# Two of four weight sums per seven-product group moved from VectorE into adding DMAs

## The chip, the cores and the metric

The kernel runs on one core of a Trainium2 chip. The time is the device time of one execution in microseconds (us), the median of several runs. Its engines are TensorE (PE, matmuls; PEld its weight loads), VectorE (DVE), ScalarE (ACT), GpSimd (POOL) and SyncE (SP, which here only issues DMAs); 16 DMA engines move data between HBM and the on-chip memory SBUF. Each engine takes its instructions in a fixed order, written when the kernel is built, and waits on semaphores for the others.

## The reference

One layer of an encoder, on 512 tokens of width 2048, in float32:

```python
h = layer_norm(x, ln_in_g, ln_in_b)
z = h @ w_in                       # then latent attention and a gated recurrence: y_attn, y_lru
y = concat([y_attn, y_lru]) @ w_out
h = layer_norm(ALPHA * h + y, ln1_g, ln1_b)
f = square(relu(h @ w_up)) @ w_down        # w_up 2048 x 8192, w_down 8192 x 2048
h = layer_norm(ALPHA * h + f, ln2_g, ln2_b)
```

The change concerns the last product pair, `w_up` and `w_down`.

## The kernel before

**Arithmetic.** TensorE multiplies in a rounded format, so every float32 operand is split into a high part (ScalarE rounds it, L159) and a low part (VectorE subtracts the high part from the operand, L160). One product is then three chains of matmuls: high x high, high x low, low x high. `split` does it for operands, `wsplit` (L839) for weight blocks of 128 x 1024, with the tiles `whi` (3 buffers) and `wlo` (2 and, every third time, 1 more). A `wsplit` is traced at a priority 100 instructions earlier than its place (`PO2`), so that it is put ahead of its product.

**Groups of seven products.** Most of `w_up` and `w_down` goes through a Strassen-Winograd scheme on 2 x 2 blocks: `winograd` (L878) computes a 256 x 512 piece of the result with seven block products in place of eight. The operand sums (tiles B11, B21, B22, T1, T2, T3, X4, each with a high part h and a low part l) are made once per stage and once per chunk; the weight sums are made in every group. A group loads its four weight blocks, slabs 0 to 3, as a11, a21, a22, a12 with plain DMAs on SP (`wload`, L860 to 864, 512 KB each) and forms on VectorE, in place, by `tt` (L876, tile `raw`): a11 - a21 (L891, product T3), a21 + a22 (L894, T1), a22 - (a11 - a21) (L899, T2) and a12 minus that (L903, B22). The products run in the order B11, T3, T1, X4, B21, B22, T2, each 24 matmuls (8 x 3, L866 to 873). Between them ScalarE copies the bank of B11 to s1 (L890) and that of T3 to s7 (L893) before the bank is added to, and `evac` writes the four result blocks.

**Stages.** The up projection has two pieces by the ordinary scheme and 30 groups; `up_out` (L773) then forms differences of the result blocks on VectorE and stores 1 MB to `u_dram`. The down projection has four chunks; in each the first piece is ordinary (`classic`, L760), with 7 groups behind it (6 in the last chunk, whose last piece is written apart). That is 57 groups. At the passage into a chunk `u_load` (L912) reads the operands back from `u_dram` in pieces of 512 KB and splits them, on the same queue and engines as the weights.

**Buffers.** `wraw` (L853) takes a weight block's buffer: of seven blocks in a row three from the pool `wr` (3 buffers, shared with the ordinary pieces) and four from the pool `ws` (4 buffers). The pool `ws` is opened at L835 in the space of R, which is freed at L834 once L827 to 833 have formed the operand sums from it.

**Order.** The framework orders each engine's instructions by priority and by when it expects their inputs, and gives buffers to tiles as they come free; a DMA's issue waits on its queue for its buffer. GpSimd issues no DMA in this kernel.

Of the kernel before, what the change touches and what calls it, by code (L numbers as in the profile page):

```python
# [9 lines left out]
F32 = mybir.dt.float32  # L10
F32R = mybir.dt.float32r
I32 = mybir.dt.int32
AF = mybir.ActivationFunctionType
ALU = mybir.AluOpType
# [4 lines left out]
P = 128  # L19
# [23 lines left out]
PO1, PO2 = 100, 100  # L43
# [5 lines left out]
def body(tc, x, pos, vecs, consts, w_in, w_uq, w_kn, w_v, w_rg, w_out, w_up, w_down, out):  # L49
    nc = tc.nc  # L50
    V, A, T, G = nc.vector, nc.scalar, nc.tensor, nc.gpsimd
# [106 lines left out]
    def split(f, hi, lo):  # L158
        A.activation(hi, f, AF.Copy)  # L159
        V.tensor_tensor(out=lo, in0=f, in1=hi.bitcast(F32), op=ALU.subtract)  # L160
# [363 lines left out]
    for step, what in enumerate(ORDER):  # L524
        c, k = what[0], int(what[1])
# [245 lines left out]
            evac(n, acc)  # L771

    def up_out(ch, o):  # L773
        V.tensor_tensor(out=o[:, 4:7:2, :], in0=o[:, 1:4:2, :], in1=o[:, 0:2, :], op=ALU.subtract)
        V.tensor_tensor(out=o[:, 5, :], in0=o[:, 3, :], in1=o[:, 4, :], op=ALU.subtract)
        V.tensor_tensor(out=o[:, 7, :], in0=o[:, 2, :], in1=o[:, 5, :], op=ALU.subtract)
        nc.sync.dma_start(out=u_dram[ch // 8][:, ch % 8], in_=o)
# [6 lines left out]
    def o_tile():  # L784
        return o_p.tile([P, 8, HS], F32, tag="uo", name="uo", bufs=2)
# [14 lines left out]
    for th in range(2):  # L800
        for k in range(KT):
            b, ws = BLK[k // 8, th], slice((k % 8) * P, (k % 8 + 1) * P)
            for n in range(NG):
                wh, wl = sl[n, k // 8]
                o = acc[n][:, TH[th]]
# [3 lines left out]
    for n in range(NG):  # L809
        up_evac(os_[n // 2], n % 2, acc[n])  # L810
        if n % 2 == 1:
            up_out(n // 2, os_[n // 2])
    for n in range(NG, 2 * NCL):
        if n % 2 == 0 and n > NG:
            os_.append(o_tile())
        acc = ps.tile([P, S], F32, tag="mm", name="mm", bufs=3)
        for hf in range(2):
            wh, wl = slab(w_up[2 * n + hf])
            for j in range(8):
                mm_blocks(acc, wh, wl, hf, j)  # L820
        up_evac(os_[n // 2], n % 2, acc)
        if n % 2 == 1:
            up_out(n // 2, os_[n // 2])
# [3 lines left out]
    for g in range(0, 8, 4):  # L827
        b11, b12 = hv[:, g:g + 4, :HS], hv[:, g:g + 4, HS:]
        b21, b22 = hv[:, 8 + g:12 + g, :HS], hv[:, 8 + g:12 + g, HS:]
        for o, x, y, n in ((b11, b12, b11, "T1"), (b12, b22, b12, "T3"), (b22, b22, b11, "T2"),  # L830
                           (b21, b21, b22, "X4")):
            V.tensor_tensor(out=o, in0=x, in1=y, op=ALU.subtract)
            split(o, oph[n][:, g:g + 4, :], opl[n][:, g:g + 4, :])
    free(r_p)  # L834
    ws_p = pool("ws")  # L835
# [3 lines left out]
    def wsplit(f, n):  # L839
        woff[0] = (32, 0) if n in ("T3", "T1") else FAR  # L840
        with tc.high_priority(offset=PO2):
            w = wsplit_(f)
        woff[0] = FAR
        return w

    def wsplit_(f):
        hi = wtile(wr, "whi", 3)
        lon[0] += 1
        lo = wtile(wr, "wlo", 2) if lon[0] % 3 else wtile(ws_p, "wlo", 1)
        split(f, hi, lo)  # L850
        return hi, lo

    def wraw(k):  # L853
        if k % 7 < 3:
            return wr.tile([P, 1024], F32, tag="raw", name="raw", bufs=3)
        return ws_p.tile([P, 1024], F32, tag="raw", name="raw", bufs=4)

    rawn = [0]

    def wload(src):  # L860
        t = wraw(rawn[0])
        rawn[0] += 1
        nc.sync.dma_start(out=t, in_=src)
        return t

    def product(acc, w, n, first):  # L866
        wh, wl = w
        sk = dict(skip_group_check=not first)
        for j in range(8):
            ws = slice(j * P, (j + 1) * P)  # L870
            T.matmul(acc, wh[:, ws], oph[n][:, j], start=first and j == 0, stop=False, **sk)  # L871
            T.matmul(acc, wh[:, ws], opl[n][:, j], start=False, stop=False, **sk)  # L872
            T.matmul(acc, wl[:, ws], oph[n][:, j], start=False, stop=j == 7, **sk)  # L873

    def tt(o, x, y, op):
        V.tensor_tensor(out=o, in0=x, in1=y, op=op)  # L876

    def winograd(slabs, evac, hook=lambda n: None):  # L878

        a11 = wload(slabs[0])  # L880
        a21 = wload(slabs[2])
        a22 = wload(slabs[3])
        a12 = wload(slabs[1])
        bank = lambda tag, bufs: ps.tile([P, HS], F32, tag=tag, name="st_" + tag, bufs=bufs)
        half = lambda n: ws_p.tile([P, HS], F32, tag=n, name=n, bufs=2)
        a, b, c, d = bank("mm", 3), bank("sc", 2), bank("tr", 3), bank("mm", 3)
        s1, s7 = half("s1"), half("s7")
        product(a, wsplit(a11, "B11"), "B11", True)
        hook("B11")
        A.activation(s1, a, AF.Copy)  # L890
        tt(a11, a11, a21, ALU.subtract)  # L891
        product(b, wsplit(a11, "T3"), "T3", True)
        A.activation(s7, b, AF.Copy)  # L893
        tt(a21, a21, a22, ALU.add)  # L894
        product(c, wsplit(a21, "T1"), "T1", True)
        tt(s7, s7, c, ALU.add)
        product(b, wsplit(a22, "X4"), "X4", False)
        hook("X4")
        tt(a11, a22, a11, ALU.subtract)  # L899
        product(a, wsplit(a12, "B21"), "B21", False)  # L900
        hook("B21")
        evac("c11", a, None)
        tt(a12, a12, a11, ALU.subtract)  # L903
        product(c, wsplit(a12, "B22"), "B22", False)
        hook("B22")
        product(d, wsplit(a11, "T2"), "T2", True)
        tt(s1, s1, d, ALU.add)
        evac("c21", s1, b)
        evac("c12", s1, c)
        evac("c22", s1, s7)  # L910
# [13 lines left out]
    for ch in range(NCL, DFF // 256):  # L924
        o = o_tile()

        def evac(which, x, y):
            t = o[:, 2 * int(which[1]) + int(which[2]) - 3, :]
            if y is not None:
                tt(t, x, y, ALU.add)  # L930
                x = t
            A.activation(t, x, AF.Relu)
            A.activation(t, t, AF.Square)
        winograd([w_up[4 * ch + i] for i in range(4)], evac,
                 *([next_ops(0)] if ch == DFF // 256 - 1 else ()))
        up_out(ch, o)
# [150 lines left out]
```

## Time and profile before

| | |
|---|---|
| median of 3 runs | 1981.27 us (1980.73 to 1982.22) |
| the profiled execution | 1981.16 us |
| its span, first to last instruction | 1979.4 us |
| TensorE, VectorE, ScalarE, GpSimd busy | 1932.1, 1501.8, 1014.6, 18.1 us |
| granted TensorE clock, mean | 0.998 of 2.4 GHz |
| bytes by DMA | 284.19 MB, mean 144 GB/s |

Rows below that name a line, an engine and tiles read `out<-in`; L12 is line 12 of the kernel. A group's `x228 | 278.3, 1221 | 3.6` is the number of instructions, their busy time in us, the mean ns of one, and the engine's idle time ahead of them. A timeline row begins with the start in us from the span's start and the duration; in brackets stands the idle time before it and who ended it. SPq is the queue of SP.

### The profile page before, as it was taken

How to read it: one execution, taken by the hardware profiler on the slowest of the kernel's cores; microseconds unless marked ns; L12 is line 12 of the kernel's file. 1: busy time of each engine (PE TensorE's matmuls, PEld its weight loads, DVE VectorE, ACT ScalarE, POOL GpSimd, SP SyncE). 2: the span in 40 equal slices, each digit the busy share in tenths (PEclk: the TensorE clock that was granted, in tenths of full speed). 3: DMA queues.
4: the chain of work that ended last, by engine and by line, in shares of the span. 5: the costliest groups of instructions: out<-in, count | busy, mean ns of one | idle time of the engine just before them, and what ended most of it. 6: DMA issues, size and time to landing. Idle time of an engine off the chain costs nothing.

```text
span 1979.4 us, 39294 instructions
## 1 busy us (share of the span) xinstructions
PE 1932.1 (98%) x16472; PEld 1899.7 (96%) x16472; DVE 1501.8 (76%) x2151; ACT 1014.6 (51%) x1479; POOL 18.1 (1%) x20
## 2 busy tenths in 40 slices
PE   6999999999999999999999999999999999999997
PEld 6999999888999999999999999999999999999997
DVE  7666655677433598888888888888898888888895
ACT  6565566555222455555555555566464454445453
POOL 1000000000000000000000000000000000000001
PEclk9999999999999999999999999999999999999999
DMA  7222222221333345454444445486364355347332
GB/s 244 96 96 94 91 93 85 65 59 65 107 107 123 115 150 204 156 180 154 179 159 162 176 156 182 153 295 223 118 222 162 107 185 198 109 140 244 100 104 86
DMA packets 113890, 284.19 MB, mean 144 GB/s; under 512 B 10161, under 2 KB 56369, under 8 KB 109617
## 3 DMA queue, kind: packets, MB, share of 16 engines
q1 hardware_dynamic: 113712, 281.68, 41.4%
q8 instruction: 129, 2.11, 0.4%
q14 instruction: 49, 0.39, 0.1%
HBM read 234.19 MB, written 46.14 MB: 142 GB/s over the span
## 4 chain that ended last, share of the span: by engine, by line
PE 88%; DVE 4%; ACT 3%; DMA 2%; issue 2%; POOL 0%; SPq 0%; ACTq 0%; DVEq 0%; POOLq 0%
PE st_mm L871 8%; PE st_mm L872 8%; PE st_mm L873 8%; PE mm L142 7%; PE mm L141 7%; PE mm L140 7%; PE st_tr L873 5%; PE st_sc L873 5%; PE st_sc L871 5%; PE st_tr L872 5%; PE st_tr L871 5%; PE st_sc L872 5%; PE mm L756 1%; PE mm L758 1%; PE mm L757 1%
## 5 line engine op out<-in xcount | busy, mean ns | idle before, releaser
L159 ACT ACTIVATE whi<-raw 128x1024 fp32r<-128x1024 f32 x399 | 423.5, 1063 | 513.5 <-DVE raw L876 251.6
L160 DVE TENSOR_TENSOR wlo<-raw,whi 128x1024 fp32r<-128x1024 f32 x399 | 484.5, 1222 | 129.4 <-ACT whi L159 123.5
L876 DVE TENSOR_TENSOR raw<-raw 128x1024 f32<-128x1024 f32 x228 | 278.3, 1221 | 3.6
L124 DVE TENSOR_TENSOR wlo<-raw,whi 128x1024 fp32r<-128x1024 f32 (+1 forms) x128 | 141.3, 1105 | 160.9 <-PE mm L142 110.3
L121 ACT ACTIVATE whi<-raw 128x1024 fp32r<-128x1024 f32 (+1 forms) x128 | 123.0, 966 | 195.6 <-PE mm L141 160.8
L141 PE MATMUL mm<-hl,whi 128*128 128x256 f32 x704 | 195.3, 277 | 0.0
L142 PE MATMUL mm<-hh,wlo 128*128 128x256 f32 x704 | 195.0, 277 | 0.0
L140 PE MATMUL mm<-hh,whi 128*128 128x256 f32 x704 | 194.7, 277 | 0.1
L140 PEld LDWEIGHTS mm<-hh,whi 128*128 128x128 f32 x704 | 132.2, 188 | 0.3 <-ACT xp L443 0.3
L142 PEld LDWEIGHTS mm<-hh,wlo 128*128 128x128 f32 x704 | 132.2, 188 | 0.1
L141 PEld LDWEIGHTS mm<-hl,whi 128*128 128x128 f32 x704 | 132.2, 188 | 0.0
L871 PE MATMUL st_sc<-X4h,whi 128*128 128x256 f32 x456 | 126.6, 278 | 2.0 <-ACT s L893 2.0
L873 PE MATMUL st_sc<-T3h,wlo 128*128 128x256 f32 x456 | 126.5, 277 | 1.8 <-DVE wlo L160 1.8
L871 PE MATMUL st_tr<-B22h,whi 128*128 128x256 f32 x456 | 126.6, 278 | 1.0 <-ACT whi L159 1.0
L873 PE MATMUL st_tr<-B22h,wlo 128*128 128x256 f32 x456 | 126.2, 277 | 0.7 <-DVE wlo L160 0.7
L871 PE MATMUL st_mm<-B21h,whi 128*128 128x256 f32 x456 | 126.0, 276 | 0.8 <-ACT s L890 0.8
L871 PE MATMUL st_mm<-T2h,whi 128*128 128x256 f32 x456 | 126.0, 276 | 0.4 <-ACT whi L159 0.4
L872 PE MATMUL st_sc<-X4l,whi 128*128 128x256 f32 x456 | 126.3, 277 | 0.0
L873 PE MATMUL st_sc<-X4h,wlo 128*128 128x256 f32 x456 | 126.2, 277 | 0.0
L871 PE MATMUL st_sc<-T3h,whi 128*128 128x256 f32 x456 | 126.1, 277 | 0.0
L872 PE MATMUL st_sc<-T3l,whi 128*128 128x256 f32 x456 | 126.1, 277 | 0.0
L873 PE MATMUL st_mm<-B11h,wlo 128*128 128x256 f32 x456 | 126.0, 276 | 0.0
(443 smaller groups left out, 6462.3 us busy)
## 6 DMA issues: line engine op xcount, KB each, us to landing
raw<-in_w_up SPq DMA_DIRECT2D x128, 512.0 KB, 3.3
raw<-in_w_down SPq DMA_DIRECT2D x128, 512.0 KB, 3.6
u_dram<-uo SPq DMA_DIRECT2D x32, 1024.0 KB, 3.8
raw<-in_w_in SPq DMA_DIRECT2D x50, 512.0 KB, 3.2
raw<-in_w_out SPq DMA_DIRECT2D x32, 512.0 KB, 3.2
X4l<-u_dram SPq DMA_DIRECT2D x18, 512.0 KB, 5.3
x<-in_x SPq DMA_DIRECT2D x8, 512.0 KB, 7.1
h_dram<-hf SPq DMA_DIRECT2D x32, 128.0 KB, 2.1
```

Of the source, the lines that this page charges most:

```text
L121: A.activation(hi[:, :w], raw[:, :w], AF.Copy)
L124: V.tensor_tensor(out=lo[:, :w], in0=raw[:, :w], in1=hi[:, :w].bitcast(F32), op=ALU.subtract)
L140: T.matmul(acc[:, c], wh, xh[:, c], start=first and t == 0, stop=False)
L141: T.matmul(acc[:, c], wh, xl[:, c], start=False, stop=False)
L142: T.matmul(acc[:, c], wl, xh[:, c], start=False, stop=last and t == 1)
L159: A.activation(hi, f, AF.Copy)
L160: V.tensor_tensor(out=lo, in0=f, in1=hi.bitcast(F32), op=ALU.subtract)
L756: T.matmul(o, wh[:, ws], oph[b][:, j], start=first and t == 0, stop=False)
L871: T.matmul(acc, wh[:, ws], oph[n][:, j], start=first and j == 0, stop=False, **sk)
L872: T.matmul(acc, wh[:, ws], opl[n][:, j], start=False, stop=False, **sk)
L873: T.matmul(acc, wl[:, ws], oph[n][:, j], start=False, stop=j == 7, **sk)
L876: V.tensor_tensor(out=o, in0=x, in1=y, op=op)
```

## The change

In each group the sum for T3 is now formed with the other sign, as a21 - a11: ScalarE writes -a11 into a tile of its own, s3n, and a DMA on GpSimd's queue adds slab 2 onto it. The sum for T1 is formed in a tile s1w: a plain DMA on SP loads slab 2, and a DMA on GpSimd's queue adds slab 3. The operand T3 changes its sign to match (B12 - B22), and T2's sum becomes a22 + s3n. Two `tt` of the group go. The raw buffers go from 3 + 4 to 3 + 2, and s3w and s1w have 2 each. `up_out` writes its first pair of differences with two instructions in place of one, for the sign. The descriptor scratch of GpSimd's DMAs is set to 8192 bytes per partition.

```diff
     def up_out(ch, o):
-        V.tensor_tensor(out=o[:, 4:7:2, :], in0=o[:, 1:4:2, :], in1=o[:, 0:2, :], op=ALU.subtract)
+        V.tensor_tensor(out=o[:, 4, :], in0=o[:, 1, :], in1=o[:, 0, :], op=ALU.subtract)
+        V.tensor_tensor(out=o[:, 6, :], in0=o[:, 1, :], in1=o[:, 3, :], op=ALU.subtract)
...
-        for o, x, y, n in ((b11, b12, b11, "T1"), (b12, b22, b12, "T3"), (b22, b22, b11, "T2"),
+        for o, x, y, n in ((b11, b12, b11, "T1"), (b12, b12, b22, "T3"), (b22, b22, b11, "T2"),
...
     def wraw(k):
-        if k % 7 < 3:
+        if k % 5 < 3:
             return wr.tile([P, 1024], F32, tag="raw", name="raw", bufs=3)
-        return ws_p.tile([P, 1024], F32, tag="raw", name="raw", bufs=4)
+        return ws_p.tile([P, 1024], F32, tag="raw", name="raw", bufs=2)
...
         a11 = wload(slabs[0])
-        a21 = wload(slabs[2])
+        s3n = ws_p.tile([P, 1024], F32, tag="s3w", name="s3w", bufs=2)
+        with tc.high_priority(offset=PO2):
+            A.activation(s3n, a11, AF.Copy, scale=-1.0)
+        G.dma_start(out=s3n, in_=slabs[2], accum_op=ALU.add)
+        s1w = ws_p.tile([P, 1024], F32, tag="s1w", name="s1w", bufs=2)
+        nc.sync.dma_start(out=s1w, in_=slabs[2])
+        G.dma_start(out=s1w, in_=slabs[3], accum_op=ALU.add)
         a22 = wload(slabs[3])
         a12 = wload(slabs[1])
...
-        tt(a11, a11, a21, ALU.subtract)
-        product(b, wsplit(a11, "T3"), "T3", True)
+        product(b, wsplit(s3n, "T3"), "T3", True)
         A.activation(s7, b, AF.Copy)
-        tt(a21, a21, a22, ALU.add)
-        product(c, wsplit(a21, "T1"), "T1", True)
+        product(c, wsplit(s1w, "T1"), "T1", True)
...
-        tt(a11, a22, a11, ALU.subtract)
+        tt(a11, a22, s3n, ALU.add)
...
-    nc = _bacc.Bacc("TRN2", target_bir_lowering=False, num_devices=1)
+    nc = _bacc.Bacc("TRN2", target_bir_lowering=False, num_devices=1, dynamic_dma_scratch_size=8192)
```

## Rows read from the trace of the kernel before

**Rows 1.** The page: busy time and share by engine, and the DMA queues.
```profile
PE 1932.1 (98%) x16472; PEld 1899.7 (96%) x16472; DVE 1501.8 (76%) x2151; ACT 1014.6 (51%) x1479; POOL 18.1 (1%) x20
...
q1 hardware_dynamic: 113712, 281.68, 41.4%
```

**Rows 2.** Stretches: busy us (instructions) by engine, granted clock, DMA share, GB/s.
```profile
740.00:1300.00 560.00, 560.00 (x4933) 560.00 (x4932) 470.25 (x557) 304.58 (x494) 0.00 (x0) 1.00 0.48 169
1300.00:1330.00 30.00, 27.80 (x239) 27.19 (x239) 28.00 (x32) 25.92 (x37) 0.00 (x0) 1.00 0.97 344
1460.00:1490.00 30.00, 28.77 (x253) 28.57 (x253) 28.55 (x34) 22.30 (x23) 0.00 (x0) 1.00 0.96 325
1500.00:1600.00 100.00, 100.00 (x883) 100.00 (x882) 85.43 (x105) 42.35 (x49) 0.00 (x0) 1.00 0.34 112
1620.00:1650.00 30.00, 28.80 (x248) 28.21 (x248) 28.72 (x33) 19.98 (x21) 0.00 (x0) 1.00 0.96 332
1770.00:1810.00 40.00, 39.44 (x344) 39.05 (x344) 37.27 (x43) 25.07 (x27) 0.00 (x0) 1.00 0.88 303
```

**Rows 3.** Waits of TensorE in 740 to 1900: us in total, times, longest.
```profile
PE st_sc L871 <- ACT s L893: 2.0, 3, 1.2
PE st_sc L873 <- DVE wlo L160: 1.8, 2, 1.0
PE st_tr L871 <- ACT whi L159: 1.0, 1, 1.0
PE st_mm L871 <- ACT s L890: 0.8, 1, 0.8
PE st_tr L873 <- DVE wlo L160: 0.7, 2, 0.4
PE st_mm L871 <- ACT whi L159: 0.4, 1, 0.4
PE mm L758 <- DVE wlo L124: 0.3, 1, 0.3
```

**Rows 4.** The costliest groups of the page: high parts and weight sums.
```profile
L159 ACT ACTIVATE whi<-raw 128x1024 fp32r<-128x1024 f32 x399 | 423.5, 1063 | 513.5 <-DVE raw L876 251.6
...
L876 DVE TENSOR_TENSOR raw<-raw 128x1024 f32<-128x1024 f32 x228 | 278.3, 1221 | 3.6
```

**Rows 5.** Timeline of TensorE: starts of B11, T3 and the next group's B11.
```profile
1105.02 0.28 PE L871 MATMUL st_mm<-B11h,whi 128*128 128x256 f32 x1
...
1107.75 0.28 PE L871 MATMUL st_sc<-T3h,whi 128*128 128x256 f32 x1
...
1124.10 0.28 PE L871 MATMUL st_mm<-B11h,whi 128*128 128x256 f32 x1
```

**Rows 6.** The same group: ScalarE's high part of T3, and SP's later issues.
```profile
1103.40 1.06 ACT L159 ACTIVATE whi<-raw 128x1024 fp32r<-128x1024 f32 x1 [1.90 <-DVE raw L876]
...
1113.72 0.33 SPq L777 DMA_DIRECT2D u_dram<-uo  x1
1117.23 1.48 SPq L863 DMA_DIRECT2D raw<-in_w_up  x2
```

**Rows 7.** Landing times: all loads of L863, its five of 740.5-746, all of L917.
```profile
DMA to landing us min/median/max: 3.0/3.3/9.1
...
DMA to landing us min/median/max: 3.7/5.3/7.6
...
DMA to landing us min/median/max: 3.4/5.5/8.5
```

**Rows 8.** Start of the stage: SP's wait, the last reader of R, T3's first matmul.
```profile
SPq L863 <- DVE X4l L160: 5.3, 1, 5.3
...
739.33 1.22 DVE L160 TENSOR_TENSOR X4l<-R,X4h 128x1024 fp32r<-128x1024 f32 x1
...
745.23 0.28 PE L871 MATMUL st_sc<-T3h,whi 128*128 128x256 f32 x1
```

**Rows 9.** Timeline of TensorE in the passage at 1300: B21 ahead of X4.
```profile
1301.28 0.28 PE L871 MATMUL st_tr<-T1h,whi 128*128 128x256 f32 x1
...
1304.94 0.39 PE L871 MATMUL st_mm<-B21h,whi 128*128 128x256 f32 x1 [0.77 <-ACT s L890]
...
1305.28 0.33 PE L871 MATMUL st_sc<-X4h,whi 128*128 128x256 f32 x1
```

## The prediction, made before the change was run

> **What bounds the kernel now.** The first view is the page's busy table [rows 1]: TensorE is busy for 98% of the span, VectorE for 76%, ScalarE for 51%, GpSimd for 1%; the DMA engines stand at 41.4% of their time. The change takes work from VectorE and gives some to ScalarE, GpSimd's queue and the DMA engines, so the question is where TensorE waits for VectorE at all. The second view, the table of stretches [rows 2], answers it by stage. The 30 seven-product groups of the up projection fill 740 to 1300 us and a little more; there TensorE is busy for 560.00 of 560.00 us, at a granted clock of 1.00, with VectorE at 84% (470.25 / 560) and the DMA engines at 0.48. The quiet part of the down projection (1500 to 1600) is as full: 100.00 of 100.00. Both stretches hold the same 8.8 matmuls per us, with the DMA share at 0.48 and at 0.34, so the matmul rate does not follow the traffic. Only the four passages into a new 2048-column chunk show idle TensorE: 2.20 us in 1300-1330, 1.23 in 1460-1490, 1.20 in 1620-1650, 0.56 in 1770-1810, with the DMA engines at 0.88 to 0.97 and VectorE at 93 to 96%.
>
> The third view, TensorE's waits in 740-1900 [rows 3], gives the most that can be won: 2.0 + 1.8 + 1.0 + 0.8 + 0.7 + 0.4 + 0.3 = 7.0 us, or 0.35% of the time. Of it 1.8 + 0.7 + 0.3 = 2.8 us wait for VectorE (a low part that is late), 4.2 us for ScalarE (a high part, or the copies of s1 and s7). VectorE's share of the whole kernel is therefore the wrong number to read; these 7.0 us are the right one.
>
> **The change, part by part.** *Removed from VectorE:* two of the four 1024-wide sums in each of 57 groups; 228 of them took 278.3 us, 1221 ns each [rows 4], so 114 x 1.22 = 139 us. They lie beside a TensorE that does not stop, so outside the passages they are worth nothing.
>
> *Added to ScalarE:* one 1024-wide negated copy per group, 57 x 1.06 us (the row of the same shape, 1063 ns [rows 4]) = 61 us. ScalarE is busy for 304.58 of 560 us in the up stage [rows 2], 10.4 of the 19.08 us of a group (1105.02 to 1124.10 [rows 5]); with 11.4 it is still hidden. Without that cover it would cost 61 us.
>
> *Added to DMA:* two adding transfers of 512 KB per group, on GpSimd's queue. The third and fourth plain loads stay (slab 2 now goes to s1w). A plain 512 KB load occupies all 16 engines for 512 KB / (169 GB/s / 0.48) = 1.5 us [rows 2]. No adding transfer is in this trace. Bounds: 1.5 us, as a plain load, and 4.5, if its two reads and its write followed one another; I take 3.0, because its reads are doubled and its writes are not. That is 6 us per group (3 to 9), a share of 0.31: the up stage goes from 0.48 to 0.79 (0.64 to 0.95), the quiet down stage from 0.34 to 0.65. Both stay below 1, so I cost it at nothing there.
>
> *Added wait, steady groups.* ScalarE's negation waits for a11's load, and behind it in ScalarE's queue stand the splits, the evacuations and the copies of s1 and s7; the adding DMA waits for the negation, T3's split for the adding DMA. SP issues a load as soon as a buffer is free [rows 6]: the one at 1117.23 follows the low part that frees a12's buffer, and with five buffers for three loads it is that of a11 two groups on. Its landing at the median of 3.3 us [rows 7] gives 1120.5; negation 1.06, adding transfer 6, so s3n is whole by about 1128. T3's high part is written 4.35 us ahead of its product (1103.40 against 1107.75 [rows 5, 6]); two groups on, that write falls at 1103.40 + 2 x 19.08 = 1141.6. Some 14 us are spare, and s1w, loaded when T1's split frees its buffer, has more. Cost: nothing, covered by that lead. If the lead were gone, each late microsecond would cost 57.
>
> *Start of the stage.* The first group has no lead. Its pool ws reuses the space of R, and SP stood 5.3 us for the last reader of R, the low part of X4 that ends at 740.55 [rows 8]. Before, a11, a21 and a22 of that group lay in the other pool, and T3 began at 745.23 [rows 8]. Now the negation cannot write before 740.6: it ends at 741.7, the adding DMA lands 3.0 to 9.1 us later (the fastest and slowest plain loads of this line [rows 7]), the high part takes 1.06, the low part 1.22, less the 0.23 of two matmuls that need only the high part. I take 6.0 us: the five loads issued at that moment landed in a median of 5.3 [rows 7], and half a load's 1.5 us comes on top for the second read. 741.7 + 6.0 + 1.06 + 0.99 = 749.7, which is 4.5 us late (1.5 to 7.6); T1's sum lands while T3 runs. The Trainium skill (DMA: Bandwidth & Descriptors, Anatomy of one DMA) fits a software-issued DMA with 2.0 us plus bytes / 436 GB/s; with two reads that would be an estimate of 4.4 us, and the start would cost 2.9 and the sum 1.6 less. No row here shows such a DMA; I stay with the rows, since the loads of that moment were slower than a lone one.
>
> *Four passages.* Here the operands of the next chunk are read back, in 512 KB pieces that land after 3.4 to 8.5 us [rows 7], on engines that are already at 0.88 to 0.97. The adding DMAs of the groups behind the passage fall into it and share the same engines: 6 us per group, of which I let half delay the operand loads, 3 us. Against it VectorE has two sums less, 2.4 us, on a path where it is 93 to 96% busy. Net +0.6 each, +2.4 for four (bounds: all 7.0 us of waits gone, or +3 each). The Trainium skill (DMA: Bandwidth & Descriptors, Issuing engines are not separate DMA queues) says the same against this change: transfers from another queue run on the same 16 engines and save only issue time. By it alone, with the whole 6 us counted, the four passages would cost +14.4 and the sum 12 more; the rows of the passages show only 0.6 to 2.2 us of waits at full DMA load, so I keep half.
>
> *Small edits.* The outer sum of the up groups becomes two instructions; some 0.1 us of VectorE, under cover. Buffers: 7 raw become 5 plus 2 + 2; no cost while the lead holds. The smaller scratch moves addresses by a whole 8 KB. The nearest row is the matmul rate, 8.8 per us in two stages that use different tiles [rows 2]: 0, up or down.
>
> **Sum.** Steady groups 0, start +4.5, passages +2.4: +6.9. The profiled execution took 1981.16 us (span 1979.4, 1.8 around it), 0.1 below the median of the three runs, so the forecast is 1981.2 + 6.9 = 1988 us.
>
> **Rivals.** A measurement of this kernel can tell about 0.2%, 4 us, from no change; the bounds are 1977.3 and 1985.2.
>
> *Even.* TensorE fills the start with another product (B21 needs neither sum, 2.7 us), or the adding DMA lands at 3.0; start +1.5, passages 0: 1983. For it: in the passage at 1300 TensorE did begin B21 right after T1, ahead of X4 [rows 9]. Against it: the loads at 740.6 were slow [rows 7]. Chance 0.30.
>
> *Faster.* VectorE's relief clears the passages: its own 2.8 us, and most of the 4.2 behind ScalarE. It decides if the operand loads are not slower than now. 1981.2 + 1.5 - 7.0 = 1976. Against it: ScalarE's waits there are for landings, which get no earlier. Chance 0.14.
>
> *DMA-bound groups.* If an adding transfer holds the engines for 6 us, an up group needs 4 x 1.5 + 2 x 6 + 3 (its 1 MB store) = 21 us against 19.08, and the 30 groups become 30 x 1.9 = 58 us longer: 2040. It decides from (19.08 - 9) / 2 = 5 us per transfer, just above my upper bound of 4.5. The Trainium skill (Collectives: The Full Stack, The bandwidth ceiling) says that an add in the DMA costs its two reads and not the arithmetic, so half the rate; by that this rival falls, and no run here shows it yet. Chance 0.10.
>
> **How the numbers follow.** The forecast, start and passages each a few us, has 0.46. Faster 0.14, same 0.30, slower 0.46 + 0.10 = 0.56. The range runs from 1977, which keeps the upper half of the faster case, to 2006: start 7.6 plus passages 4 x 3 is 2001, and a few us more for groups that now and then run late. Half of *faster* and all but a corner of *DMA-bound groups* stay outside, under 0.2.
>
> **What would show it.** Right: 1500-1600 again with 100.00 busy; a wait of TensorE for T3's split near 745 to 750; DMA share near 0.8 in the up stage; GpSimd's DMA landing in 4 to 7 us; VectorE some 130 us less busy with next to nothing to show for it. Wrong: waits of ScalarE for GpSimd's DMA in every group, an up stage longer than 560 us, or passages without any wait of TensorE.

## The result, and the profile after

| | before | after |
|---|---|---|
| median (4 runs each, same chip) | 1981.54 us (1980.73 to 1982.22) | 2043.03 us (2040.61 to 2043.74) |
| ratio after / before | | 1.0299, 95% interval [1.0287, 1.0312] |
| span of the profiled execution | 1979.4 us | 2042.0 us |
| granted TensorE clock, mean | 0.998 | 0.985 |

The change costs 3.0% by the ratio in the table; the medians lie 61.5 us apart, and their quotient, 1.0310, lies within the interval. The forecast was +7. The direction held, the size did not, and 2043 lies outside the range of 1977 to 2006. The profiled executions differ by 2042.0 - 1979.4 = 62.6 us.

The page of the changed kernel, to be laid beside [rows 1 and 4]:

```profile
PE 1954.9 (96%) x16472; PEld 1917.9 (94%) x16472; DVE 1389.2 (68%) x2069; ACT 1066.9 (52%) x1536; POOL 117.9 (6%) x134
...
q1 hardware_dynamic: 113712, 281.68, 40.3%
q0 software_dynamic: 16416, 59.78, 17.1%
...
L884 ACT ACTIVATE s3w<-raw 128x1024 f32<-128x1024 f32 x57 | 60.5, 1061 | 125.9 <-DMA raw<-in_w_up 66.4
```

VectorE lost 1501.8 - 1389.2 = 113 us of busy time and ScalarE gained 52, and the time went the other way. A new queue, q0, holds the 114 adding transfers. Each occupies the 16 DMA engines for 0.171 x 2042 / 114 = 3.06 us, and a plain 512 KB load for 0.403 x 2042 / (281.68 MB / 0.524 MB) = 1.53 us. An adding transfer takes twice the engine time, the 3.0 us of the prediction. The Trainium skill (Collectives: The Full Stack, The bandwidth ceiling) says that an add in the DMA costs its two reads, so half the rate; the trace agrees, 1.53 against 3.06.

Stretches of the changed kernel (us, busy time with instructions of PE, PEld, DVE, ACT, POOL, then granted clock, DMA share, GB/s):

```profile
740.00:760.00 20.00, 9.64 (x80) 9.14 (x79) 7.56 (x9) 5.92 (x8) 2.83 (x3) 0.78 0.80 235
760.00:900.00 140.00, 139.99 (x1210) 139.88 (x1211) 99.54 (x125) 81.61 (x129) 13.06 (x15) 0.98 0.78 212
900.00:1300.00 400.00, 396.77 (x3475) 395.16 (x3474) 290.53 (x371) 232.16 (x368) 35.80 (x41) 1.00 0.78 220
...
1360.00:1390.00 30.00, 22.87 (x183) 22.38 (x183) 16.55 (x18) 14.79 (x21) 2.69 (x4) 0.89 0.90 274
...
1500.00:1600.00 100.00, 92.66 (x789) 92.06 (x788) 73.50 (x85) 52.91 (x58) 7.85 (x9) 0.97 0.80 224
```

The up stage was full before [rows 2]. Now TensorE is idle for half of its first 20 us, then full again, then short of 400 by 3.2 us; the DMA share is 0.78, as forecast (0.79). The next hole comes at 1360, behind the first passage.

TensorE's waits in 740 to 1960 of the changed kernel (us in total, times, longest):

```profile
PE st_sc L872 <- ACT whi L159: 14.7, 3, 9.9
PE st_sc L874 <- DVE wlo L160: 12.4, 8, 6.1
PE st_tr L872 <- ACT whi L159: 10.6, 3, 4.4
PE st_tr L874 <- DVE wlo L160: 4.6, 5, 1.5
PE st_sc L872 <- ACT s L899: 2.2, 2, 1.4
...
```

With two more lines of 0.9 us together they sum to 45.4 us against 7.0 before [rows 3], and are few and long: three waits take 14.7 us. Nearly all stand at products T3 (bank sc) and T1 (bank tr), whose weights come from adding transfers; it is shown below that what they wait for is not always that transfer.

**The first group.** Timeline of the changed kernel, 744 to 759:

```profile
744.04 1.06 ACT L884 ACTIVATE s3w<-raw 128x1024 f32<-128x1024 f32 x1 [2.26 <-DVE X4l L160]
744.08 0.33 SPq L887 DMA_DIRECT2D s1w<-in_w_up  x1
...
744.46 0.43 SPq L864 DMA_DIRECT2D raw<-in_w_up  x1
...
744.93 0.42 SPq L887 DMA_DIRECT2D s1w<-in_w_up  x1
...
745.40 0.43 SPq L864 DMA_DIRECT2D raw<-in_w_up  x1
...
745.72 1.08 POOL L885 DMA_DIRECT2D s3w<-in_w_up  x1 [44.14 <-ACT s3w L884]
...
757.59 1.06 ACT L159 ACTIVATE whi<-s3w 128x1024 fp32r<-128x1024 f32 x1 [10.17 <-DMA s3w<-in_w_up]
...
758.70 0.58 PE L872 MATMUL st_sc<-T3h,whi 128*128 128x256 f32 x1 [9.86 <-ACT whi L159]
```

As the pool comes free, four plain loads are issued at once; the negation takes 1.06 us, and the adding transfer is issued last, behind all four. TensorE ends B11 at 748.84 and stands 9.86 us. Landing times of the adding transfers onto s3w, all 57 of them, and who waited:

```profile
who waited for it (us, times):
  ACT whi L159: 24.8, 4
...
DMA to landing us min/median/max: 5.2/5.5/11.8
```

The 11.8 is this first one; 30 of the 57 land in 5.2 to 5.6, the others between. Four loads ahead at 1.53 us of the engines plus the median of 5.5 make an estimate of 11.6; the second sum's adding transfer, which ran beside the end of this one from 748.16, is not in it. ScalarE waited for only four of the 57.

**The clock.** The stretches of the weight stage in which the granted clock stood at 0.50 of 2.4 GHz, that is at 1.2 (columns as above):

```profile
751.40:765.10 13.70, 5.89 (x26) 5.60 (x27) 4.72 (x4) 4.48 (x6) 1.73 (x2) 0.50 1.05 249
1369.20:1376.00 6.80, 3.89 (x16) 3.60 (x17) 5.51 (x6) 5.50 (x9) 0.87 (x1) 0.50 0.65 224
1399.90:1406.70 6.80, 6.10 (x29) 5.85 (x28) 5.21 (x6) 4.67 (x9) 0.87 (x1) 0.50 0.52 165
1546.70:1553.50 6.80, 5.46 (x25) 5.47 (x26) 5.07 (x6) 2.20 (x5) 0.25 (x1) 0.50 0.52 157
1710.50:1717.30 6.80, 5.55 (x24) 5.26 (x25) 5.46 (x6) 2.36 (x4) 0.87 (x1) 0.50 0.49 151
1874.30:1881.10 6.80, 5.31 (x25) 5.32 (x26) 4.30 (x5) 1.58 (x3) 0.51 (x1) 0.50 0.40 125
```

Each begins in or right behind a wait of TensorE of 2.9 to 9.9 us; the kernel before has none in this stage. TensorE is busy for 32.2 us in them at half speed, which costs 16.1 us. Waits (45.4 - 7.0 = 38.4) and clock (16.1) make 54.5 of the 59.1 us lost in the groups.

**Where the groups grew.** How much longer than before each part is, from the starts of B11 of the 57 groups in the profiled executions (us; the four parts "chunk" are the passage and the groups behind it). Runs other than the changed kernel are told below. Most profiled executions lie within 2 us of their run's median; that of e2 (2006.00 us) is 6.0 above it and that of e11 (2002.67) 5.6 below, so their rows hold that much more or less than the medians.

| run | before the groups | groups 1-2 | rest of up | chunk 1 | 2 | 3 | 4 | span |
|---|---|---|---|---|---|---|---|---|
| changed kernel | 3.5 | 13.5 | 7.3 | 13.6 | 9.3 | 7.5 | 8.0 | +62.6 |
| e1 VectorE sums | 1.1 | 5.0 | 4.0 | -0.5 | 0.5 | -1.0 | -0.3 | +8.6 |
| e2 nine groups by VectorE | 4.3 | 3.3 | 13.4 | 5.9 | -0.3 | -1.0 | -0.7 | +24.9 |
| e3 copies, no add | 1.1 | 10.9 | 3.2 | 7.2 | 0.8 | 2.2 | 0.4 | +25.7 |
| e4 first sum by DMA | 0.6 | 10.6 | 26.4 | 10.6 | 9.8 | 8.4 | 9.7 | +76.1 |
| e5 second sum by DMA | 2.5 | 11.1 | 1.7 | 0.8 | 0.5 | -1.2 | 3.2 | +18.3 |
| e6 negation on GpSimd | 0.5 | 11.3 | 0.0 | 17.8 | 5.0 | 2.6 | -1.0 | +36.4 |
| e8 = e2 and e6 | 1.5 | 6.9 | 0.0 | 6.6 | 0.2 | -0.5 | -1.4 | +13.2 |
| e9 adding transfer first | 1.5 | 10.2 | 9.8 | 10.8 | 7.4 | 9.9 | 8.1 | +57.8 |
| e10 = e1, early buffer | 0.2 | 1.9 | 2.4 | 0.1 | -0.7 | -0.4 | 1.3 | +4.7 |
| e11 negation, no DMA sum | 1.0 | 3.3 | 14.0 | 0.8 | 0.5 | 2.7 | -0.8 | +21.5 |
| e12 = e6, early buffer | 1.7 | 10.8 | 0.0 | 15.7 | 4.9 | 0.2 | 10.8 | +44.0 |
| e13 eleven by VectorE | 2.3 | 0.1 | 0.0 | -0.1 | -0.4 | -1.0 | 1.9 | +2.7 |

The column ahead of the groups changes by some us between executions of the same instructions (the changed kernel's has two stretches of 3.4 us at half clock, from 72.1 and 502.2) and is no work of the change. In the changed kernel 7.3 us lie in the rest of the up stage, in steps of 0.2 to 2.1 us, nearly all at every fifth group, with 0.0 between them. One of them in the timeline:

```profile
1106.57 1.06 ACT L884 ACTIVATE s3w<-raw 128x1024 f32<-128x1024 f32 x1 [4.21 <-DMA raw<-in_w_up]
...
1107.53 1.05 ACT L159 ACTIVATE whi<-s3w 128x1024 fp32r<-128x1024 f32 x1
...
1107.93 0.87 POOL L885 DMA_DIRECT2D s3w<-in_w_up  x1 [11.64 <-ACT s3w L884]
...
1109.89 0.39 PE L874 MATMUL st_sc<-T3h,wlo 128*128 128x256 f32 x1 [0.76 <-DVE wlo L160]
```

The negation of the *next* group waits 4.21 us for its load at the head of ScalarE's queue; behind it stands T3's high part of *this* group, whose s3n is long there. ScalarE's list of waits shows that this is the rule; it hurts only where T3's split is next in line:

```profile
ACT s3w L884 <- DMA raw<-in_w_up: 66.4, 27, 4.6
ACT s3w L884 <- DMA raw<-in_w_down: 57.2, 23, 5.0
```

In 50 of 57 groups the negation stands for its load. The first group behind the first passage shows the start once more:

```profile
1356.13 1.06 ACT L884 ACTIVATE s3w<-raw 128x1024 f32<-128x1024 f32 x1 [2.77 <-DMA raw<-in_w_down]
...
1357.49 0.88 POOL L885 DMA_DIRECT2D s3w<-in_w_down  x1 [45.55 <-ACT s3w L884]
...
1368.45 1.06 ACT L159 ACTIVATE whi<-s3w 128x1024 fp32r<-128x1024 f32 x1 [7.85 <-DMA s3w<-in_w_down]
...
1369.56 0.58 PE L872 MATMUL st_sc<-T3h,whi 128*128 128x256 f32 x1 [4.58 <-ACT whi L159]
```

The block to be negated came late (the operands and the residual were loading), the transfer was issued at 1357.49 and its result was split 10.96 us later. In the second group TensorE stands 3.40 us for T1's high part; its sum had landed at 1394.8, but the write at 1398.50 stood in ScalarE's order behind loads of the residual, which took up to 12.3 us (6.3 before).

The other three passages are not like this. There the last piece of the operand X4, 512 KB on SP's queue, runs beside two or three adding transfers and lands after 13.2, 11.7 and 11.0 us, where the same piece took 5.1, 5.2 and 5.6 before. The landing times of all operand pieces of the changed kernel (before: the last row of [rows 7]), and the last passage:

```profile
DMA to landing us min/median/max: 3.5/5.5/13.2
```

```profile
1861.26 1.06 ACT L159 ACTIVATE whi<-s3w 128x1024 fp32r<-128x1024 f32 x1 [2.13 <-PE mm L757]
...
1872.28 1.06 ACT L159 ACTIVATE X4h<-X4l 128x1024 fp32r<-128x1024 f32 x1 [8.96 <-DMA X4l<-u_dram]
...
1873.37 1.23 DVE L160 TENSOR_TENSOR X4l<-X4l,X4h 128x1024 fp32r<-128x1024 f32 x1 [8.38 <-ACT X4h L159]
1874.52 1.22 DVE L160 TENSOR_TENSOR wlo<-s3w,whi 128x1024 fp32r<-128x1024 f32 x1
...
1875.79 0.58 PE L874 MATMUL st_sc<-T3h,wlo 128*128 128x256 f32 x1 [6.06 <-DVE wlo L160]
```

T3's weights were there: its adding transfer had landed 40.9 us before its high part was written at 1861.26. Its low part stood in VectorE's order behind that of X4, and X4 behind its load. At the second and third passage TensorE has no such wait at T3 (none above 0.5 us) but stands 4.35 and 2.86 us for the high part of T1, which is behind the same piece of X4 in ScalarE's order; the second sum itself landed only some 0.5 to 1 us before that piece, so these rows do not say which of the two would have been enough.

### The profile page after: what moved, and what is told of

Read it like the earlier page. It is cut to its first block, busy times and chain, and to the rows that moved or that the text cites. A ratio compares the mean times of both kernels' runs of the same rounds, so it can differ in the third digit from the quotient of the medians.

```text
span 2042.0 us, 39507 instructions
## 1 busy us (share of the span) xinstructions
PE 1954.9 (96%) x16472; PEld 1917.9 (94%) x16472; DVE 1389.2 (68%) x2069; ACT 1066.9 (52%) x1536; POOL 117.9 (6%) x134
## 3 DMA queue, kind: packets, MB, share of 16 engines
q1 hardware_dynamic: 113712, 281.68, 40.3%
## 4 chain that ended last, share of the span: by engine, by line
PE 79%; DMA 8%; DVE 5%; ACT 4%; issue 3%; POOL 0%; SPq 0%; POOLq 0%; ACTq 0%; DVEq 0%
PE mm L142 7%; PE mm L141 7%; PE mm L140 7%; PE st_mm L872 6%; PE st_mm L873 6%; PE st_mm L874 6%; PE st_sc L874 5%; PE st_sc L872 5%; PE st_sc L873 5%; PE st_tr L874 5%; PE st_tr L872 5%; PE st_tr L873 5%; DMA X4l<-u_dram 2%; DMA raw<-in_w_up 2%; DVE wlo L160 1%
## 5 line engine op out<-in xcount | busy, mean ns | idle before, releaser
L160 DVE TENSOR_TENSOR wlo<-raw,whi 128x1024 fp32r<-128x1024 f32 x285 | 346.9, 1223 | 172.6 <-ACT whi L159 169.8
L159 ACT ACTIVATE whi<-raw 128x1024 fp32r<-128x1024 f32 x285 | 299.7, 1058 | 268.8 <-PE st_mm L873 106.6
L872 PE MATMUL st_sc<-T3h,whi 128*128 128x256 f32 x456 | 129.8, 285 | 14.8 <-ACT whi L159 14.7
L872 PE MATMUL st_tr<-T1h,whi 128*128 128x256 f32 x456 | 129.5, 284 | 10.6 <-ACT whi L159 10.6
L874 PE MATMUL st_tr<-T1h,wlo 128*128 128x256 f32 x456 | 129.8, 285 | 3.5 <-DVE wlo L160 3.5
L873 PE MATMUL st_tr<-T1l,whi 128*128 128x256 f32 x456 | 129.1, 283 | 0.0
L884 ACT ACTIVATE s3w<-raw 128x1024 f32<-128x1024 f32 x57 | 60.5, 1061 | 125.9 <-DMA raw<-in_w_up 66.4
```

The lines of the kernel that those rows point to most:

```text
L884: A.activation(s3n, a11, AF.Copy, scale=-1.0)
```

## The experiments

The diffs below are against the changed kernel and show what each edit comes to.

**The theory:** an adding transfer is only late where it has no lead: in the first group of the stage and the first ones behind each passage, where it lands in 9 to 12 us behind other loads; the clock falls behind these gaps; and the negation blocks ScalarE's queue in every fifth group. **Rivals:** the adding traffic costs DMA time in every group; the new buffers do it; GpSimd's queue and the chain of waits do it, not the add. The medians of the kernel before were 1983 to 1986 us beside these runs, so ratios are compared.

**e1: VectorE makes all sums in the new layout.**

```diff
-        with tc.high_priority(offset=PO2):
-            A.activation(s3n, a11, AF.Copy, scale=-1.0)
-        G.dma_start(out=s3n, in_=slabs[2], accum_op=ALU.add)
...
-        G.dma_start(out=s1w, in_=slabs[3], accum_op=ALU.add)
...
+        tt(s3n, s1w, a11, ALU.subtract)
         product(b, wsplit(s3n, "T3"), "T3", True)
...
+        tt(s1w, s1w, a22, ALU.add)
         product(c, wsplit(s1w, "T1"), "T1", True)
```

> All 114 adding transfers and the 57 negations are taken out: VectorE makes both sums again, with the changed kernel's tiles, signs and rings of buffers kept (five raw buffers, two each of s3w and s1w). Theory (the loss is the adding transfers' lateness where they have no lead, and the clock that falls behind those gaps): the time goes back to that of the kernel before, 1981 to 1986 us; no granted clock below full in the up stage. Rival, the smaller ring and the regrouped layout are the cost: stays at 2030 to 2043.

Measured 1.0027 [1.0016, 1.0039], 1989.75 us. The layout is not the cause: nine tenths of the loss go with the adding transfers and the negations. The time is some 4 us above what the theory gave, with the kernel before at 1984.67 beside it; 5.0 us are left in the first groups, and one stretch of 3.4 us at half clock, at 749.8, which the theory did not have (e10).

**e2: VectorE sums in the nine groups without lead.**

```diff
+        v = g == 0 or (g >= 30 and (g - 30) % 7 < 2)
-        G.dma_start(out=s3n, in_=slabs[2], accum_op=ALU.add)
+        if not v:
+            G.dma_start(out=s3n, in_=slabs[2], accum_op=ALU.add)
...
+        if v:
+            tt(s3n, s1w, a11, ALU.subtract)
```

(The negation and the second sum follow the same condition.)

> VectorE makes both sums in 9 of the 57 groups only: the first of the up stage and the first two behind each of the four classic passages; the other 48 keep their adding transfers and negations. Theory: the loss sits in these 9 groups (13.6 us at the start and 31.7 of the 37.5 us at the passages, both with the half-clock stretches behind their gaps) and 7 us in the hiccups of every fifth group, so 1985 to 1994 us. Rival, adding transfers cost DMA time in every group or the ring of buffers is too small: the 48 groups keep 48/57 of the loss, 2030 to 2035 us. Rival, the lateness only moves to the next group with an adding transfer: 2010 to 2043.

Measured 1.0085 [1.0067, 1.0102], 2000.01 us. 48 of 57 groups kept their adding transfers, and 0.0214 of the 0.0299 is gone; so the traffic in every group is not the cost. Some of the lateness did move. The second group behind the first passage is still 6.3 us long, though VectorE makes its sums: ScalarE stands there for the loads of the residual (tile R), the last of which land in 11 to 12 us (6.3 before) while the next group's transfers run beside them; the copy of T3's bank stands behind them, X4's product waits 3.1 us for that copy, and 3.4 us at half clock follow. And the rest of the up stage grew from 7.3 to 13.4 in the profiled execution. Hence 2000 and not 1985 to 1994.

**e3: the transfers on GpSimd's queue copy and do not add.**

```diff
-        G.dma_start(out=s3n, in_=slabs[2], accum_op=ALU.add)
+        G.dma_start(out=s3n, in_=slabs[2])
...
-        G.dma_start(out=s1w, in_=slabs[3], accum_op=ALU.add)
+        G.dma_start(out=s1w, in_=slabs[3])
```

> The 114 transfers stay on GpSimd's queue with all their waits but only copy: the additions of slab 2 onto the negated block and of slab 3 onto slab 2 are left out. Theory as to size (an adding transfer takes the DMA engines 3.06 us against 1.53 and lands in 5.2 to 5.6 us alone): half of the lateness goes, the chain of load, negation, issue and landing stays, so the gaps at the start and at the passages fall from 10 to some 6 us and the time to 2005 to 2030 us. Rival, the wait chain and GpSimd's queue are all of it: stays at 2038 to 2045. Rival, the double reading is all of it: 1983 to 1990.

Measured 1.0117 [1.0101, 1.0133], 2006.88 us, at the low end of what the theory gave. The queue's share and the landings onto s3w in this run:

```profile
q0 software_dynamic: 16416, 59.78, 8.8%
```

```profile
DMA to landing us min/median/max: 3.4/3.6/9.6
```

8.8% of 2005 us over 114 is 1.55 us each, a plain load's. The first one still lands in 9.6 us, which is 4 x 1.53 + 3.6 = 9.7: there the loads ahead count, not the add, and the first groups keep 10.9 of 13.5 us. Behind the passages the loss falls from 38.3 to 10.6 us: there the doubled time counts. Of the 0.0299, 0.0182 go with the second read and 0.0117 stay with the chain and the layout.

**e4: only the first sum by an adding transfer; e5: only the second.**

```diff
-        G.dma_start(out=s1w, in_=slabs[3], accum_op=ALU.add)
...
+        tt(s1w, s1w, a22, ALU.add)
         product(c, wsplit(s1w, "T1"), "T1", True)
```

> In all groups only the first sum (slab 2 onto the negated slab 0) is an adding transfer; VectorE makes the second (slab 2 plus slab 3). Theory: the T3 product waits for this transfer behind a load and a negation, so it carries most of the loss, but with half of the adding traffic it lands sooner, 8 us instead of 11.8 at the start: 2005 to 2030 us. Rival, the loss belongs to both alike: 2010 to 2014. Rival, the second sum's transfer carries it: 1985 to 1995.

```diff
-        with tc.high_priority(offset=PO2):
-            A.activation(s3n, a11, AF.Copy, scale=-1.0)
-        G.dma_start(out=s3n, in_=slabs[2], accum_op=ALU.add)
+        nc.sync.dma_start(out=s3n, in_=slabs[2])
...
+        tt(s3n, s3n, a11, ALU.subtract)
         product(b, wsplit(s3n, "T3"), "T3", True)
```

> In all groups only the second sum (slab 3 onto slab 2) is an adding transfer; VectorE makes the first from a slab 2 loaded once more, and no block is negated. Theory (the late one is the first sum's transfer, which stands behind a load and a negation; the second sum is wanted 2.7 us later and needs no other engine): start some 5 us, passages 0 to 2 each, 1990 to 2005 us. Rival, both sums carry it alike: 2010 to 2020. Rival, the amount of adding traffic decides, whichever sum it is: about 2040.

Measured: e4 1.0369 [1.0352, 1.0386], 2058.05 us; e5 1.0083 [1.0068, 1.0098], 2001.08 us. e4 was expected below the changed kernel and came out above it. At the passages the sizes are as the theory has them: the groups right behind them are 28 us longer with the first sum alone, 4 with the second alone, and 40 with both. But e4 loses 26.4 us in the up stage, and some 10 in later groups of the chunks, of the kind that its timeline shows:

```profile
1031.93 1.22 DVE L877 TENSOR_TENSOR s1w<-s1w,raw 128x1024 f32<-128x1024 f32 x1 [5.29 <-DMA raw<-in_w_up]
1033.08 1.22 DVE L160 TENSOR_TENSOR wlo<-raw,whi 128x1024 fp32r<-128x1024 f32 x1
...
1034.35 0.39 PE L874 MATMUL st_mm<-B11h,wlo 128*128 128x256 f32 x1 [3.04 <-DVE wlo L160]
```

VectorE's second sum waits 5.29 us for slab 3 with the low part of B11 behind it: the same fault as the negation's, on another engine. The framework's order put that sum there; why it did so in e4 and not in e1 was not tried. e5, which came out within what the theory gave, loads a fifth block in every group and so tells nothing of the start.

**e6: the negation on GpSimd.**

```diff
-            A.activation(s3n, a11, AF.Copy, scale=-1.0)
+            G.tensor_scalar_mul(s3n, a11, -1.0)
```

> The changed kernel with its 57 negations on GpSimd instead of ScalarE. Theory (in every fifth steady group the negation of a later group waits for its load at the head of ScalarE's queue, with the high part of T3's weights behind it): the 7.2 us that the up stage loses in those groups fall under 2; the start and the passages stay as they are or grow by what GpSimd's negation is longer than 1.06 us, in some six places: 2035 to 2055 us. Rival, the fifth group is late because its slab is late whoever negates it: the same groups lose the same 7 us.

Measured 1.0164 [1.0149, 1.0180], 2017.10 us, 26 us under the changed kernel: more than expected. Stretches of e6 (columns as above):

```profile
780.00:1300.00 520.00, 520.00 (x4581) 520.00 (x4581) 392.51 (x490) 288.19 (x463) 130.63 (x82) 1.00 0.77 221
```

520.00 of 520.00: the steps of every fifth group are gone, with all 114 adding transfers still there and the DMA share at 0.77. GpSimd's negation is slow, 3.0 us in the median for ScalarE's 1.06, and costs TensorE nothing here: nothing urgent stands behind it. It is not free for VectorE: the 93 instructions of 1024 columns that overlap a negation take 1.35 us in the mean and up to 2.06, the others 1.22; the up stage hides that. The passages fell too, from 38.3 to 24.4 us, which I had not expected. That the negation stood in ScalarE's way there is not shown by it: with the same negation e12 has 31.6.

**e8: e2 and e6 together.**

> Both edits together: VectorE makes both sums in the first group of the up stage and in the first two behind each classic passage, and GpSimd negates in the other 48. Theory: the 9 groups save what they saved alone (2043 to 2000 us), and of the 15 us that the up stage then still lost in steady groups most goes: 1985 to 1993 us. Rival, the steady groups' loss is the slab's lateness: 1998 to 2004.

Measured 1.0048 [1.0031, 1.0065], 1994.23 us, 1 us above what the theory gave; the up stage is full again from 780 (0.0 in the table). Two places are left, the first groups (6.9) and the second group behind the first passage (6.4), with the wait told under e2.

**e9: the loads of the first groups behind the adding transfer.**

```diff
-        nc.sync.dma_start(out=s1w, in_=slabs[2])
-        G.dma_start(out=s1w, in_=slabs[3], accum_op=ALU.add)
-        a22 = wload(slabs[3])
-        a12 = wload(slabs[1])
+        q = G if g < 2 or (g >= 30 and (g - 30) % 7 < 2) else nc.sync
+        q.dma_start(out=s1w, in_=slabs[2])
+        a22 = wload(slabs[3], q)
+        a12 = wload(slabs[1], q)
+        G.dma_start(out=s1w, in_=slabs[3], accum_op=ALU.add)
```

> The changed kernel, but in the first two groups of the up stage and behind each passage the plain loads of slab 2, 3 and 1 are issued from GpSimd behind the adding transfer of the first sum, so that this one has fewer loads ahead of it. Theory (its 11.8 us at the start are its own 5.2 to 5.6 plus the plain loads issued just before it, at 1.5 us of the DMA engines each): it lands in 6 to 8 us, TensorE's gap at the start falls from 10.1 to 4 to 6 us, part of it comes back at the second sum's product; 2025 to 2038 us. Rival, an adding transfer is slow in itself when it has no lead: landing stays over 10 us and the time at 2040 to 2045.

Measured 1.0271 [1.0250, 1.0292], 2039.19 us. With two loads ahead in place of four the first transfer landed in 7.8 us (11.8 before; the sum of loads ahead and the median landing gives 8.6) and TensorE's first wait was 5.5 us in place of 9.9, as expected; of these 4.3 us 1.0 came back at later products (10.2 in the table for 13.5). At the passages 2 us were won. The ratio is 0.0028 lower, about the least that the theory gave: the order of the loads sets the landing, but saves little, as the loads put back are then late themselves.

**e10: e1, with the first group's slab 2 in an early buffer.**

```diff
+        if g == 0:
+            s1w = wload(slabs[2])
+        else:
             s1w = ws_p.tile([P, 1024], F32, tag="s1w", name="s1w", bufs=2)
             nc.sync.dma_start(out=s1w, in_=slabs[2])
```

> VectorE makes both sums in every group, as in the run with vector sums alone, and in the first group slab 2 is loaded into a buffer of the early ring instead of the pool that comes free only at 741.7 us. Theory (some 5 of the 13.6 us at the start are this placement: slab 2's load cannot start before the pool is free, with or without an adding transfer): the step of the first group falls from 5.0 to under 1 us, and the time from 1.0027 times the kernel before to 0.998 to 1.001. Rival, the start waits for something else in the new layout: stays at 1.002 to 1.004.

Measured 1.0021 [1.0012, 1.0030], 1987.41 us. The step of the first group fell from 5.0 to 0.1 us, as the theory had it, and 1.9 us came up in the second; the total cannot tell it from e1 (the intervals overlap), did not reach the 1.001 that I had allowed and lies where the rival put it. The placement is shown in the group, not in the time.

**e11: the negation, but no adding transfer.**

```diff
-        G.dma_start(out=s3n, in_=slabs[2], accum_op=ALU.add)
...
+        tt(s3n, s3n, s1w, ALU.add)
         product(b, wsplit(s3n, "T3"), "T3", True)
```

(The second sum as in e1.)

> VectorE makes both sums in every group, but the first onto a block that ScalarE wrote negated ahead of time, as in the changed kernel; no adding transfer. Theory (the steady groups' hiccups come from the negation standing at the head of ScalarE's queue for its load; the start and the passages from adding transfers): about 7 us over the run with vector sums alone, in groups of period five: 1.005 to 1.009 times the kernel before. Rival, a negation only hurts where its adding transfer is late too: 1.002 to 1.004. Rival, the negation on ScalarE is behind the passages also: 1.012 to 1.02.

Measured 1.0120 [1.0102, 1.0138], 2008.22 us: the negation on ScalarE alone costs 0.9% over e1, more than the 7 us expected, and as much as one rival gave; but not where that rival had it. It is 14.0 us in the up stage (4.0 in e1) and little behind the passages. TensorE's longest item in e11:

```profile
PE st_sc L872 <- ACT s L906: 10.7, 15, 0.9
```

Fifteen short waits for the copy of the bank to s7 (L906); in e1 the same wait sums to 4.6 us. The copy does not stand right behind the negation. At 902 the negation had waited 3.53 us for its load, VectorE's first sum 2.82 for the negation, ScalarE's evacuations 2.52 for VectorE's sums behind it, and the copy stood behind the evacuations: a way over VectorE that the changed kernel does not have. So e11 shows that a late negation is felt, not that its 0.9% are in the changed kernel. At the passages it costs little without late transfers.

**e12: e6, with the early buffer of e10.**

> The changed kernel with both adding transfers everywhere, the negations on GpSimd, and in the first group slab 2 loaded into a buffer of the early ring, where slab 3 is then added to it. Theory (the start's 11.3 us with GpSimd's negation are 5 of placement and 6 of an adding transfer behind other loads): the first group's step falls to 5 to 8 us, the passages keep their 27: 1.012 to 1.015 times the kernel before. Rival, the first sum's transfer alone sets the start: step 10 to 12, 1.016 to 1.018.

Measured 1.0206 [1.0187, 1.0225], 2025.65 us; the first groups keep 10.8 us. The rival was right as to the step: as long as the first sum comes by an adding transfer, that one sets the start, and the placement of slab 2 shows only where VectorE makes the sum. The total lies above what both gave. Chunk 4 lost 10.8 us here and -1.0 in e6: the last piece of X4 landed there in 9.9 us in this run and in 3.6 in e6, with T3's low part behind it as in the changed kernel. The early buffer shifts the ring by one block; that this moved the piece into the adding transfers was not tried.

**e13: adding transfers in steady groups alone, negations on GpSimd.** As e8 with the early buffer, and VectorE's sums in the second group and in the third behind the first passage as well: 11 groups, and 46 that keep their transfers.

```diff
+        v = g < 2 or (g >= 30 and (g - 30) % 7 < 2) or g == 32
```

> Adding transfers and GpSimd's negations in 45 steady groups alone; VectorE makes both sums in 12 groups: the first two of the up stage, the first two behind each passage, the third behind the first one, and the one before the first passage's end that this numbering takes with it, if any; the first group's slab 2 goes into a buffer of the early ring. Theory (an adding transfer with lead, and no wait on ScalarE's queue, costs nothing, though it holds the DMA engines twice as long): the time of the run with vector sums and the early buffer, 1.000 to 1.004 times the kernel before, with 0.0 us steps in the groups that keep their transfers. Rival, the lateness moves on to the first groups that keep theirs: 1.006 to 1.012.

(The issue rows count 28 + 18 = 46 of each transfer.) Measured 1.0001 [0.9992, 1.0010], 1983.98 us against 1983.09. Queue, stretch and TensorE's waits of e13:

```profile
q0 software_dynamic: 13248, 48.24, 13.8%
```

```profile
780.00:1300.00 520.00, 520.00 (x4581) 520.00 (x4580) 392.34 (x493) 289.14 (x464) 126.61 (x79) 1.00 0.76 220
```

```profile
PE st_sc L874 <- DVE wlo L160: 2.8, 2, 1.9
PE st_sc L872 <- ACT s L911: 2.2, 2, 1.3
...
```

Four fifths of the adding traffic are still there, and the time is that of the kernel before. The waits sum to 7.6 us, 1.3 of them behind the last group, against 7.0 [rows 3]. No run beat the kernel before; e13 is level with it. Against e10, which has VectorE's sums in every group of the same layout, it is a little faster (1.0021 [1.0012, 1.0030], with 2.4 us in the rest of the up stage where e13 has 0.0): the likeliest reading, not tried by itself, is that VectorE's relief pays for what the layout costs, and for no more.

## Why the prediction was right in direction and wrong in size

- **Removed sums, worth nothing.** Right against the kernel before: VectorE is busy for 113 us less, and the up stage was full already. Only in the new layout, which costs 0.2% by itself (e10), do they show (e13).
- **The price of an adding transfer, 3.0 us of the engines.** Right: 3.06. The rival *DMA-bound groups* gave 2040, close to what was measured, and is still wrong: it needed 6 us per transfer and 1.9 us in every group, and the steady groups grow by 0.00 (e6, e13). A matching total is no evidence; the place of the loss is.
- **Steady groups, cost nothing.** Right for the transfer: issued at 1107.93, it lands 5.3 us later, and the next group splits its block at 1123.70, so 10.5 us are spare there, and 10.0 to 17.5 in the groups of the up stage behind the first, for the 14 forecast. Wrong for the queue: the prediction named what stands behind the negation and costed it at nothing, since the *block* had time. But the negation itself waited for its load in 50 of 57 groups, up to 5.0 us, and T3's high part of another group stood behind it: 7.3 us in the up stage. Moving the negation to GpSimd took this to 0.0 (e6).
- **Start, +4.5.** This step failed in its size: 13.5. The landing was taken as 6.0, from the median of the five loads of that moment [rows 7]; the adding transfer is issued behind four of them, and took 11.8. The row's largest value, 7.6, was the nearer one, and loads ahead times engine time plus the median landing gives 11.6. The Trainium skill's fit with two reads (DMA: Bandwidth & Descriptors, Anatomy of one DMA), the estimate of 4.4 us, lies below even the fastest landing, 5.2. The rest, some 3 us, is the clock.
- **Passages, +2.4.** This step failed most: 38.3 us. It priced what the transfers do to the operand loads, 3 us a passage, and took VectorE's relief of 2.4 off. At three of the four passages that was the right wait with the wrong size: the last piece of X4 landed 8.1, 6.5 and 5.4 us later than before, with the splits of T1 or T3 behind it, and the slow clock behind that. What the relief gave back does not show. At the first passage it is the start once more, a first group without lead, which the prediction did not price there, and behind it the residual's loads, late in the same way. e4 and e5 show that it takes the first sum's transfers (28 us against 4; the piece of X4 lands in 10.7, 10.2 and 8.7 us in e4, in 4.9, 4.9 and 7.5 in e5), e3 that the doubled engine time counts here (10.6 in place of 38.3; 7.6, 8.5 and 6.1), e13 that VectorE's sums in these groups end it (3.5, 4.6 and 6.8).
- **The clock.** Not in the sum at all; half-speed stretches behind the gaps cost 16.1 us. In e11, whose waits in the groups are 1.6 us at most, the trace has no such stretch there.
- **What would show it.** DMA share near 0.8, the wait for T3 in the first group (to 758.7 where 745 to 750 was written), a landing of 5.5 us in the median and VectorE's relief (113 for some 130) came; 1500 to 1600 with 100.00 busy did not (92.66, since the second passage now falls into it). Of the marks against it the longer up stage came true; waits for GpSimd's DMA in every group did not (4 of 57), nor passages without a wait. It had no mark for passages with long waits, which is what came.

## What to carry to other kernels

A sum by an adding DMA costs nothing where its result lands ahead of its use (in e13 by 1.8 us at the least), and all of its lateness where it has no lead: list every place where the pipeline starts anew, and price each as loads ahead times engine time, plus the landing of one. List beside it the other loads that are wanted at that moment, and what stands behind them in each engine's order: at three passages it was such a load that came late. An instruction that waits for a load does its harm through what stands behind it; an idle engine that takes three times as long (GpSimd's 3.0 us against 1.06) was the better place for it. And a gap of TensorE may cost more than itself: add the slow stretch behind it.

## What the runs showed of the hardware

- An adding transfer of 512 KB holds the 16 DMA engines for 3.06 us, a copy of the same size on the same queue for 1.55; they land in 5.5 and 3.6 us (medians of the s3w rows).
- Behind four plain loads they land in 11.8 and 9.6 us: the loads' 6.1 us of engine time come on top almost whole. Behind two loads it was 7.8 (e9), 0.8 less than this sum gives.
- A plain operand load of 512 KB on SP's queue with two or three adding transfers of GpSimd's queue beside it landed in 13.2, 11.7 and 11.0 us; the same pieces in the kernel before in 5.1, 5.2 and 5.6.
- VectorE's instructions on 128x1024 take 1.22 us, and 1.35 in the mean, 2.06 at most, while GpSimd negates a block of that size (e6).
- Six waits of TensorE, or pairs of them, of 2.9 us and more each came with a stretch of 6.8 us at 1.2 GHz, the longest with one of 13.7 us; four of the six stretches began within the wait.
